# A two-layer hybrid decoder trunk: eight constants loaded after the third pair of tiles, and the first stage's small steps re-set

## The chip, the core and the metric

The kernel runs on one core of one Trainium2 chip. The metric is the device time of one execution in microseconds (us). Shown for the kernel before are three timed runs, with their median, and one further execution that was profiled.

## What is computed

```python
c_act = silu(c)
for l in range(2):                                  # DEPTH
    shift, scale, gate = split(c_act @ w_mod[l] + b_mod[l])
    h = rms_norm(x, pre_gain[l]) * (1 + scale) + shift
    proj = h @ w_in[l]          # 3088 columns: aq ak av ag | rq rk rv rg | gq gk gv gg ga
    a = window_attention(rope(aq), rope(ak), av, sinks[l]) * silu(ag)   # 8 heads, window 128
    r = rms_norm(retention(rot(rq), rot(rk), rv)) * silu(rg)           # 4 heads, chunks of 128
    g = rms_norm(gla(gq, gk, gv, log_sigmoid(ga @ gate_w + gate_b) / 16), gn) * silu(gg)
    y = concat(a, r, g) @ w_out[l]
    x = x + gate * rms_norm(y, post_gain[l])
```

x is 1 x 1024 x 1024 in fp32. All products are fp32 in accuracy.

## The kernel before, in words

The 1024 tokens are cut into eight tiles of 128 (`t` = 0 to 7), which are worked on in four pairs (`p`). An accurate fp32 product is made of three fast ones: each operand is split into a high part (rounded to fp32r) and a low part (the rest), and high x high, low x high and high x low are summed in PSUM. A projection of one tile onto one unit of weights (256 columns, or 272 for `gg`, which carries the 16 gate columns `ga`) is therefore 3 x 8 = 24 products (`accum`, L161 in the trace, since all products go through one helper).

Weights live in an arena of seven places. `load` (from L463 on) brings a unit in four chunks of 256 KB into a staging tile (`st`, five buffers), makes the high part (L145 on ScalarE or L147 on VectorE; in the first two units L484 and L488, on ScalarE) and then the low part (L491, on GpSimd or VectorE).

The first stage goes like this. The modulation of layer 0 (`mod_first`) multiplies `c_act` by two 1024 x 1024 blocks of `w_mod`, in two halves `hh` of eight steps `k`: the shift on TensorE, one row of 512 columns per step, and the scale on VectorE (L326). `finish` turns the row and the VectorE sum into columns, one small product per 128 values; for the first half that is done in the second half's step `FIN`. Meanwhile `x` tiles 0 and 1 come in over ScalarE's queue (`xk`), are squared and summed on ScalarE (L541), get their reciprocal root on GpSimd (L543 to L545, `rstd_early`), are scaled (L602), transposed on TensorE (L176), modulated (L647, L648) and split into high and low parts. The first unit `gg` is split beside this. As soon as the modulation stands, `gg` is multiplied with tiles 0 and 1 (`begin`, `complete`).

Tiles 2 and 3 come next (`pre` with `soon`): squares at L581, reciprocal root in `rstd2` (a sum at L534 and a scale at L528 on VectorE, a power at L529 on GpSimd), scaling at L600 (ScalarE) and L602 (VectorE), eight transposes a tile (L176), modulation at L622 (ScalarE) and L624 (VectorE), high part at L628 (ScalarE), low part at L629 (GpSimd for the first half of a tile, VectorE for the second). Tiles 4 to 7 follow by the same lines (`pre_first`); their `x` is loaded by the Sync queue at L686.

Then `layer(0)` runs the gates: for each pair first `gg`, then `rg` (`do_gates`). Each gate gives a SiLU (L1007 on ScalarE, L1009 on VectorE) that is written to DRAM, and `gg` also gives the gate logits (L1015, a transpose, L1024). After the gates come the decays of the gated linear attention (`gla_log`, `gla_decays`), retention, the attention projections, and the output projection; then layer 1.

Three things set the order of the work.

- On TensorE the order is the order of the program. The program is written as jobs on a planned clock: every product advances `clk`, and a job that yields `L["pf1"]` is taken up again when the clock is that many us further (`pump`, called every seven products). So the table `L` decides after how many products a transpose or a small product is put in.
- On the other engines, the Sync queue (SP) among them, a scheduler of the language picks the order: of the instructions that are ready, the one that stands first in the program. It looks over the whole program. On the chip every engine then takes its own list strictly in order.
- `tc.issue_after` pins some instructions behind another one on their engine (`XF`, `GH`).

In the kernel before, the eight constants (`causal` to `cdt`, 64 KB each for the first three, 128 KB for `rmask`, 1 to 2 KB for the others) stand in the program right behind `pump()` at L756, and the attention sinks, the gate weights `gwt` and the norm gain `gncol` stand at L795 to L808, ahead of the layers. None of them is used in the gates. The VectorE steps on them are the copies at L799 and the scaling at L808.

Of the kernel before, what the change touches and what calls it, by code (L numbers as in the profile page):

```python
# [89 lines left out]
def trunk(ctx: ExitStack, tc: tile.TileContext, ins, cst, out):  # L90
# [665 lines left out]
    pump()  # L756
    causal = cload("causal")
    mask2 = cload("mask2", I32)
    curmask = cload("curmask", I32)
    rmask = cload("rmask")  # L760
    hmask = cload("hmask")
    qdec = cload("qdec")
    kdec = cload("kdec")
    cdt = cload("cdt")
    kv = {}
# [11 lines left out]
    def gla_tiles():  # L777
# [13 lines left out]
        for b in range(2):  # L791
            gz["sc"].append([gp.tile([P, 4, 129], F32, tag="smx", name=nm("sc"), bufs=SMB)[:, :, 0:P] for _ in range(2)])
            for c in range(2):
                G.memset(gz["sc"][b][c], 0.0)
    sink8 = cp.tile([P, 2, 8], F32, name="sink8")  # L795
    sinkn = small(16)
    nc.sync.dma_start(sinkn, sinks.rearrange("(o a) b -> o (a b)", o=1).to_broadcast((P, 16)))
    for l in range(DEPTH):
        V.tensor_copy(sink8[:, l].rearrange("p (m r) -> p m r", r=2),  # L799
                      sinkn[:, 8 * l:8 * l + 8].rearrange("p (r m) -> p m r", r=2))  # L800
    gwt = cp.tile([32, 2, P], F32, name="gwt")
    V.memset(gwt, 0.0)
    for l in range(DEPTH):
        nc.sync.dma_start(gwt[0:16, l, :], gw_in[l])
        nc.sync.dma_start(gwt[16:17, l, :], gb_in[l:l + 1, :])
    for j in range(2):
        nc.sync.dma_start(gncol[64 * j:64 * j + 64, :], gn_in.rearrange("a b -> b a"))
    V.tensor_scalar(gncol, gncol, 0.5, None, ALU.mult)  # L808

# [503 lines left out]
    def layer(l):  # L1313
# [24 lines left out]
        for n in ((1, 1, 1, 1), (3, 1))[l]:  # L1338
            p0 = gates_done[l]
            for name in ("gg", "rg"):  # L1340
                for p in range(p0, p0 + n):
                    do_gates(name, p)
            if l == 0 and p0 == 0:
                load(l, "rq")
            gates_done[l] += n

        job(mod_all(l, (2,)))
# [162 lines left out]
TURN = ("AV", "AV")  # L1510
L = {"tt1": 5.71, "tt2": 6.96, "tb1": 28.02, "tb2": 0.05, "pf3": 12.62, "pf1": 6.69, "pf2": 4.0, "mod1": 4.3, "mod2": 2.4, "mod3": 17.69, "mod4": 5.8, "mod5": 0.09, "mod6": 0.05, "pre1": 7.43, "kv1": 8.84, "kv2": 2.31, "aq1": 7.17, "aq7": 7.95, "ag1": 5.62, "aq2": 2.4, "aq6": 6.2, "aq3": 11.35, "aq4": 7.54, "aq5": 4.01, "hn1": 8.14, "hn2": 3.76, "gz1": 10.47, "gz2": 13.49, "gl1": 4.43, "gd3": 16.57, "gc1": 1.21, "gc2": 1.95, "gc3": 0.65, "gc4": 3.27, "gc6": 3.2, "gc5": 4.23, "rc1": 0.73, "rc2": 2.11, "rc3": 1.31, "rc4": 2.84, "fin1": 11.68, "lay1": 0.05, "mod2@1": 2.23, "mod3@1": 16.46, "mod5@1": 3.78, "mod6@1": 3.24, "pre1@1": 10.18, "kv1@1": 3.37, "kv2@1": 0.05, "aq1@1": 5.95, "aq7@1": 6.81, "ag1@1": 8.3, "aq2@1": 2.07, "aq6@1": 9.39, "aq3@1": 11.0, "aq4@1": 6.32, "aq5@1": 1.76, "hn1@1": 10.35, "hn2@1": 3.59, "gz1@1": 3.83, "gz2@1": 12.55, "gl1@1": 17.99, "gd3@1": 15.63, "gc1@1": 1.6, "gc2@1": 1.95, "gc3@1": 0.47, "gc4@1": 1.87, "gc6@1": 0.05, "gc5@1": 1.38, "rc1@1": 0.12, "rc2@1": 3.46, "rc3@1": 2.6, "rc4@1": 5.99, "fin1@1": 9.35, "lay1@1": 1.23, "gc7": 0.81, "gc7@1": 0.33, "tb0": 0.05, "mod7": 1.0, "mod7@1": 1.0}
# [12 lines left out]
XM = (0, 3)  # L1524
LOG = (0,)
XF = 3
GH = (0,)
INP = 0
TT = 7
RG_V = ()  # L1530
FIN = 1

# [31 lines left out]
```

## Time and profile before

| | us |
|---|---|
| median of the 3 timed runs | 971.86 |
| lowest and highest of them | 971.38 and 972.01 |
| the profiled execution, its own time | 971.16 |
| its span, first to last instruction | 969.4 |

The mean granted TensorE clock of the profiled execution is 0.996. DMA moves 140.30 MB, 145 GB/s over the span.

How to read the views: a timeline row has its start and length in us, the engine, the line, the operation, the tile written and those read, the shape, how many instructions are merged into it (x), and in brackets how long the engine had been idle before it and what ended that. PE is TensorE, PEld its weight load, DVE VectorE, ACT ScalarE, POOL GpSimd; a q (SPq, ACTq) marks the engine's instruction queue, where DMAs are issued. A windows row has, for a stretch, the busy time and the number of instructions of PE, PEld, DVE, ACT and POOL, then the granted TensorE clock, the DMA share and GB/s.

### The profile page before, as it was taken

How to read it: one execution, taken by the hardware profiler on the slowest of the kernel's cores; microseconds unless marked ns; L12 is line 12 of the kernel's file. 1: busy time of each engine (PE TensorE's matmuls, PEld its weight loads, DVE VectorE, ACT ScalarE, POOL GpSimd, SP SyncE). 2: the span in 40 equal slices, each digit the busy share in tenths (PEclk: the TensorE clock that was granted, in tenths of full speed). 3: DMA queues.
4: the chain of work that ended last, by engine and by line, in shares of the span. 5: the costliest groups of instructions: out<-in, count | busy, mean ns of one | idle time of the engine just before them, and what ended most of it. 6: DMA issues, size and time to landing. Idle time of an engine off the chain costs nothing.

```text
span 969.4 us, 18061 instructions
## 1 busy us (share of the span) xinstructions
PE 951.3 (98%) x6513; PEld 829.4 (86%) x6513; DVE 640.2 (66%) x1525; ACT 410.1 (42%) x1119; POOL 272.5 (28%) x323
## 2 busy tenths in 40 slices
PE   6999999999999999999999999999999999999997
PEld 1799999989998877878889999998999887777886
DVE  6886857777777777655586485686776577763332
ACT  2777312354422666622455531134652166761111
POOL 3243011533430344511242110144423034441000
PEclk9999999999999999999999999999999999999999
DMA  9943314624335355677455160253222333555871
GB/s 313 320 146 110 111 56 129 187 77 112 115 102 150 98 168 180 218 242 237 172 166 172 50 180 22 83 155 92 80 86 77 120 88 105 158 174 174 261 238 65
DMA packets 124293, 140.30 MB, mean 145 GB/s; under 512 B 12734, under 2 KB 95528, under 8 KB 124204
## 3 DMA queue, kind: packets, MB, share of 16 engines
q1 hardware_dynamic: 116204, 127.43, 42.9%
q10 hardware_dynamic: 8000, 11.72, 3.4%
q8 instruction: 51, 0.84, 0.4%
q14 instruction: 38, 0.31, 0.1%
HBM read 102.42 MB, written 34.60 MB: 141 GB/s over the span
## 4 chain that ended last, share of the span: by engine, by line
PE 86%; DMA 7%; DVE 3%; issue 2%; POOL 1%; ACT 0%; SPq 0%; DVEq 0%; ACTq 0%; POOLq 0%
PE mm L161 67%; PE aux L161 15%; PE aux L176 4%; DMA wm<-in_w_mod_dram 2%; DMA t<-in_x_dram 1%; DMA st<-in_w_in_dram 1%; DMA xk<-in_x_dram 1%; DMA t<-aoS 1%; DMA st<-in_w_mod_dram 1%; POOL sm L529 1%; DVE acc L367 0%; DVE t L1292 0%; POOL arena L491 0%; DVE t L624 0%; DMA c_ident<-cst_ident_dram 0%
## 5 line engine op out<-in xcount | busy, mean ns | idle before, releaser
L161 PE MATMUL mm<-arena,arena 128*128 128x256 f32 (+2 forms) x1896 | 303.0, 315 | 1.4 <-ACT arena L628 0.7
L161 PE MATMUL mm<-arena 128*128 128x256 f32 (+2 forms) x1824 | 294.7, 317 | 0.0
L161 PEld LDWEIGHTS mm<-arena,arena 128*128 128x128 f32 x1896 | 261.8, 188 | 24.6 <-ACT arena L628 1.2
L161 PEld LDWEIGHTS mm<-arena 128*128 128x128 f32 x1824 | 255.4, 191 | 22.0 <-issue 1.2
L161 PE MATMUL mm<-arena,mx 128*128 128x512 f32 (+1 forms) x744 | 168.7, 386 | 0.0
L161 PEld LDWEIGHTS mm<-arena,mx 128*128 128x128 f32 x744 | 135.6, 188 | 29.1 <-issue 1.5
L529 POOL TENSOR_TENSOR sm<-sm,mhalf 128x4 f32<-128x4 f32 (+1 forms) x60 | 51.8, 863 | 294.8 <-DVE sm L528 285.3
L491 POOL TENSOR_TENSOR arena<-st,arena 128x512 fp32r<-128x512 f32 x55 | 80.3, 1467 | 91.3 <-ACT arena L145 34.7
L145 ACT ACTIVATE t<-aux 128x512 f32<-128x512 f32 (+1 forms) x96 | 48.7, 521 | 106.4 <-PE aux L176 44.9
L943 POOL TENSOR_TENSOR smx<-smx,sm 128x512 f32<-128x512 f32 x32 | 36.2, 1131 | 114.8 <-DVE sm L942 111.4
L491 DVE TENSOR_TENSOR arena<-st,arena 128x512 fp32r<-128x512 f32 x65 | 62.3, 969 | 4.7 <-PE mm L161 2.6
L145 ACT ACTIVATE arena<-st 128x512 fp32r<-128x512 f32 x82 | 48.5, 626 | 29.0 <-PE mm L161 13.0
L1247 ACT ACTIVATE t<-mm 128x512 f32<-128x512 f32 x30 | 17.9, 597 | 92.2 <-PE mm L161 40.3
L939 ACT ACTIVATE smx<-smx,sm 128x129 f32<-128x129 f32 x128 | 50.0, 393 | 14.0 <-DVE sm L936 13.9
L1248 DVE TENSOR_TENSOR t<-mm,modg 128x512 f32<-128x512 f32 x30 | 20.6, 689 | 48.6 <-ACT t L1247 48.5
L367 DVE SCALAR_TENSOR_TENSOR acc<-st,c_act,acc 128x512 f32<-128x512 f32 x60 | 47.3, 788 | 7.5 <-DMA st<-in_w_mod_dram 6.8
L1292 DVE SCALAR_TENSOR_TENSOR t<-t,sm,t 128x512 f32<-128x512 f32 x32 | 25.9, 846 | 39.7 <-DMA t<-xs 20.8
L176 PE MATMUL aux<-c_ident,t 128*128 128x128 f32 x288 | 45.5, 278 | 2.9 <-DVE t L602 2.9
L176 PEld LDWEIGHTS aux<-c_ident,t 128*128 128x128 f32 x288 | 34.9, 144 | 7.3 <-DVE t L602 4.2
L934 DVE COPY_PREDICATED smx<-c_curmask,aux 128x256 f32<-128x256 int32 x64 | 25.5, 447 | 15.0 <-ACT smx L145 10.4
L990 ACT ACTIVATE t<-aux 128x256 f32<-128x256 f32 x32 | 12.2, 382 | 54.1 <-PE aux L161 26.8
L995 DVE TENSOR_TENSOR t<-aux,sm 128x256 f32<-128x256 f32 x32 | 13.6, 425 | 30.8 <-POOL sm L529 30.8
(214 smaller groups left out, 1300.9 us busy)
## 6 DMA issues: line engine op xcount, KB each, us to landing
st<-in_w_in_dram SPq DMA_DIRECT2D x96, 256.0 KB
st<-in_w_mod_dram SPq DMA_DIRECT2D x64, 256.0 KB
mx<-mixS SPq DMA_DIRECT2D x30, 512.0 KB
mixS<-t SPq DMA_DIRECT2D x64, 128.0 KB
st<-in_w_out_dram SPq DMA_DIRECT2D x32, 256.0 KB
mixS<-t SPq DMA_DIRECT2D x32, 256.0 KB
wm<-in_w_mod_dram SPq DMA_DIRECT2D x12, 512.0 KB
t<-in_x_dram SPq DMA_DIRECT2D x24, 256.0 KB
```

What stands on the lines that cost most here:

```text
L145: A.activation(dst, src, AF.Copy)
L161: T.matmul(dst, lhsT, rhs, start=start, stop=stop)
L176: T.transpose(dst, src, idn)
L367: V.scalar_tensor_tensor(acc, wt, c_act[:, k:k + 1], acc, ALU.mult, ALU.add)
L491: i = (G if first == 0 and kc in LOG else V if first == 0 else eng(f"wlo{kc}")).tensor_tensor(wt[:, 1, 2 * kc:2 * kc + 2, 0:256], st, f(hi ...
L529: after[2] = G.tensor_tensor(r, r, mhalf[:, :w], ALU.pow)
L934: V.copy_predicated(sv, curmask.unsqueeze(1).to_broadcast((P, 2, P)), pv[:, :, n // P - 1, :])
L939: A.activation(sm[:, h, :], sm[:, h, :], AF.Exp, bias=mx[:, h:h + 1], accum_out=sums[:, h:h + 1])
L943: eng("pn").tensor_tensor(sm[:, :, 0:128], sm[:, :, 0:128], rs.unsqueeze(2).to_broadcast((P, 4, P)), ALU.mult)
L1247: A.activation(yg, pm, AF.Square, accum_out=ss[:, nh:nh + 1])
L1248: V.tensor_tensor(yg, pm, modg[l][:, 512 * nh:512 * nh + 512], ALU.mult)
L1292: V.scalar_tensor_tensor(xt[j], yg[j], r, xt[j], ALU.mult, ALU.add)
```

## The change

The constants, the sinks, `gwt` and `gncol` move into a function, `load_constants`, that is called in `layer(0)` when the gates of the third pair (`CL` = 2) have been put into the program. Inside it the sinks, `gwt` and `gncol` stand first and the eight constants after them. Beside this, single steps of the first stage change engine or place, and some planned times change.

```diff
@@ first stage @@
-    causal = cload("causal")
...
-    cdt = cload("cdt")
@@ ahead of the layers @@
-    sink8 = cp.tile([P, 2, 8], F32, name="sink8")
...
-    V.tensor_scalar(gncol, gncol, 0.5, None, ALU.mult)
+    causal = mask2 = curmask = rmask = hmask = qdec = kdec = cdt = sink8 = gwt = None
+
+    def load_constants():
+        nonlocal causal, mask2, curmask, rmask, hmask, qdec, kdec, cdt, sink8, gwt
+        sink8 = cp.tile([P, 2, 8], F32, name="sink8")
+        sinkn = small(16)
...
+        V.tensor_scalar(gncol, gncol, 0.5, None, ALU.mult)
+
+        causal = cload("causal")
...
+        cdt = cload("cdt")
@@ layer, gates @@
             gates_done[l] += n
+            if l == 0 and p0 == CL:
+                load_constants()
@@ settings @@
-L: "pf1": 6.69, "pf2": 4.0,  "mod1": 4.3,  "mod2": 2.4,  "gl1": 4.43, "gd3": 16.57, "fin1": 11.68, "fin1@1": 9.35, "lay1@1": 1.23
+L: "pf1": 7.45, "pf2": 3.96, "mod1": 6.36, "mod2": 2.46, "gl1": 4.5,  "gd3": 16.47, "fin1": 11.8,  "fin1@1": 9.47, "lay1@1": 0.46
+CL = 2
-RE = 1
+RE = 0
-RE2 = 0
+RE2 = 1
-LOG = (0,)
+LOG = (0, 1)
-GH = (0,)
+GH = ()
-RG_V = ()
+RG_V = (2, 3)
-FIN = 1
+FIN = 0
```

(The table `L` is one line in the program; only its changed entries are shown.) What the settings do:

- `RE`, `RE2`: with 1 the reciprocal root of a tile is made by three GpSimd steps (`rstd_early`), with 0 by two VectorE steps and one GpSimd step (`rstd2`); `RE` is for tiles 0 and 1, `RE2` for tiles 2 and 3.
- `LOG`: the chunks of the first unit `gg` whose low part is made on GpSimd instead of VectorE; chunk 1 joins chunk 0.
- `GH`: with tile 0 in it, the modulation of tile 2 is pinned behind the SiLU of tile 0's gate; empty, it is not.
- `RG_V`: the chunks of `rg` whose high part is made on VectorE instead of ScalarE; chunks 2 and 3 move.
- `FIN`: the step of the second half in which the first half's `finish` is done.

More of the change, by code (lines that the diff above doesn't have):

```diff
@@ L756, in trunk @@
     pump()
-    causal = cload("causal")
[L758 to L763, printed above, removed]
-    cdt = cload("cdt")
     kv = {}
@@ L794, in gla_tiles @@
                 G.memset(gz["sc"][b][c], 0.0)
-    sink8 = cp.tile([P, 2, 8], F32, name="sink8")
[L796 to L807, printed above, removed]
-    V.tensor_scalar(gncol, gncol, 0.5, None, ALU.mult)
+    causal = mask2 = curmask = rmask = hmask = qdec = kdec = cdt = sink8 = gwt = None
[3 more added lines that the diff above has]
+        sinkn = small(16)
+        nc.sync.dma_start(sinkn, sinks.rearrange("(o a) b -> o (a b)", o=1).to_broadcast((P, 16)))
+        for l in range(DEPTH):
+            V.tensor_copy(sink8[:, l].rearrange("p (m r) -> p m r", r=2),
+                          sinkn[:, 8 * l:8 * l + 8].rearrange("p (r m) -> p m r", r=2))
+        gwt = cp.tile([32, 2, P], F32, name="gwt")
+        V.memset(gwt, 0.0)
+        for l in range(DEPTH):
+            nc.sync.dma_start(gwt[0:16, l, :], gw_in[l])
+            nc.sync.dma_start(gwt[16:17, l, :], gb_in[l:l + 1, :])
+        for j in range(2):
+            nc.sync.dma_start(gncol[64 * j:64 * j + 64, :], gn_in.rearrange("a b -> b a"))
+        V.tensor_scalar(gncol, gncol, 0.5, None, ALU.mult)
+        causal = cload("causal")
+        mask2 = cload("mask2", I32)
+        curmask = cload("curmask", I32)
+        rmask = cload("rmask")
+        hmask = cload("hmask")
+        qdec = cload("qdec")
+        kdec = cload("kdec")
+        cdt = cload("cdt")
     def rotary(dst, src, nh, t, kind):
```

2 lines of the change are left out of this document (1 added, 1 removed).

## The prediction

> **What bounds the kernel now.** I read the page's span and engine rows first, then TensorE's waits, then windows, then the timeline from 32 to 80 us, engine by engine.
>
> ```profile
> span 969.4 us, 18061 instructions
> PE 951.3 (98%) x6513; PEld 829.4 (86%) x6513; DVE 640.2 (66%) x1525; ACT 410.1 (42%) x1119; POOL 272.5 (28%) x323
> ...
> PE aux L176 <- DVE smx L934: 0.5, 1, 0.5
> ...
> 35.00:40.00 5.00, 5.00 (x29) 4.99 (x29) 4.66 (x18) 4.13 (x13) 0.53 (x1) 0.66 0.98 300
> ...
> 80.00:969.00 889.00, 881.87 (x6083) 776.72 (x6082) 579.25 (x1386) 360.35 (x992) 247.64 (x285) 1.00 0.44 136
> ```
>
> TensorE is busy for 98% of the span, and from 80 us on for 881.87 of 889 us. So nothing in the first stage is worth anything unless TensorE comes through its own list sooner there, and all it wins there it keeps, if no later wait takes it back. A busy TensorE can still be a slow one: the rows of its products show that better than the share.
>
> ```profile
> 32.33 0.75 DVE L326 SCALAR_TENSOR_TENSOR t<-wm,c_act,t 128x512 f32<-128x512 f32 x1 [0.32 <-DMA wm<-in_w_mod_dram]
> ...
> 35.75 6.59 PE L161 MATMUL mm<-arena 128*128 128x272 f32 x39
> 42.17 0.63 PE L161 MATMUL mm<-arena,arena 128*128 128x256 f32 x4
> 42.95 0.91 PE L161 MATMUL mm<-arena,arena 128*128 128x256 f32 x3 [0.15 <-ACT arena L488]
> 43.69 2.07 PE L176 MATMUL aux<-c_ident,t 128*128 128x128 f32 x16
> 45.52 4.91 PE L161 MATMUL mm<-arena,arena 128*128 128x256 f32 x41
> 58.17 1.04 PE L176 MATMUL aux<-c_ident,t 128*128 128x128 f32 x8
> 58.96 3.91 PE L161 MATMUL mm<-arena,arena 128*128 128x256 f32 x31
> 64.85 2.37 PE L161 MATMUL mm<-arena,arena 128*128 128x272 f32 x17
> 67.43 0.77 PE L161 MATMUL mm<-arena,arena 128*128 128x272 f32 x4 [0.21 <-ACT arena L628]
> 68.73 0.65 PE L161 MATMUL mm<-arena,arena 128*128 128x272 f32 x3 [0.54 <-ACT arena L628]
> 69.22 1.03 PE L176 MATMUL aux<-c_ident,t 128*128 128x128 f32 x8
> ...
> 78.95 6.16 PE L161 MATMUL mm<-arena,arena 128*128 128x272 f32 x48
> ```
>
> Until 32.33 us the stage waits for the modulation weights, and the change takes none of their bytes away. Then TensorE loses time in three places. From 35.75 it runs 39 products of 272 columns in 6.59 us, where 48 of them take 6.16 us later (0.128 each, so 5.0 for 39): 1.6 us, at a granted clock of 0.66. From 42.17 to 43.69 it runs 7 products of 256 columns in 1.52 us; at 4.91/41 = 0.12 each they take 0.84: **0.68 us** lost to the high parts of `rg` chunks 2 and 3. The 16 transposes behind them take 45.52 - 43.69 = 1.83 us, where 8 take 58.96 - 58.17 = 0.79 and 69.22's group about the same: **0.2 us**. From 64.85 to 69.22 it runs 24 products of 272 columns in 4.37 us instead of 24 x 0.128 = 3.08: **1.29 us** lost to the high parts of tile 5.
>
> Now the chain behind tile 5, on the other engines.
>
> ```profile
> 35.33 0.46 SPq L232 DMA_DIRECT2D c_causal<-cst_causal_dram  x1
> ...
> 38.69 0.43 SPq L232 DMA_DIRECT2D c_qdec<-cst_qdec_dram  x1
> 39.55 5.14 SPq L686 DMA_DIRECT2D t<-in_x_dram  x8
> 44.73 0.43 SPq L232 DMA_DIRECT2D c_kdec<-cst_kdec_dram  x1
> ...
> 47.88 1.41 SPq L807 DMA_DIRECT2D gncol<-in_gla_norm_gain_dram  x2
> 48.42 0.47 DVE L799 COPY sink<-sm 128x8 f32<-128x8 f32 x2 [1.15 <-DMA sm<-in_attn_sinks_dram]
> 49.24 0.63 ACT L628 ACTIVATE arena<-t 128x512 fp32r<-128x512 f32 x1 [1.47 <-DVE t L624]
> ...
> 50.45 1.50 SPq L150 DMA_DIRECT2D st<-in_w_in_dram  x3
> ...
> 56.89 0.64 ACT L145 ACTIVATE arena<-st 128x512 fp32r<-128x512 f32 x1 [1.77 <-DMA st<-in_w_in_dram]
> 57.43 0.61 ACT L581 ACTIVATE t<-t 128x512 f32<-128x512 f32 x1
> ```
>
> VectorE stands still for 1.15 us for the sinks and then copies them for 0.47, with tile 2's last modulation behind it, so that ScalarE waits 1.47 us. ScalarE later stands still for 1.77 us for a chunk of `rq` weights, with the squares of tile 5 (57.43) behind that. Those chunks were issued from 50.45 on, behind nine small DMAs that held the Sync queue from 44.73 to 49.29.
>
> **The change part by part.** *The constants.* Six of them go ahead of the `x` loads (35.33 to 39.12), nine small DMAs behind. Moved back in the program they are last in line. What follows in the queue, the SiLU write-outs and `rq`, can start at 44.73 instead of 49.29, that is 4.6 us sooner, less what the write-outs wait for their data. The `rq` wait on ScalarE (1.77) then goes whole, and the stop on VectorE (1.15 + 0.47 = 1.62) too if the sinks land before their copies come up or the copies stand later. I take both: tile 5's chain comes up to 3.4 us sooner. It needs 1.29 to end the wait at 67.43, and 0.88 more because TensorE will itself be there sooner (next items): 2.17 in all, and is covered. If only one goes, 1.62 or 1.77 us is the whole gain.
>
> ```profile
> 39.85 0.15 DVE L528 TENSOR_SCALAR sm<-sm 128x1 f32<-128x1 f32 x1
> ...
> 40.98 1.29 POOL L491 TENSOR_TENSOR arena<-st,arena 128x512 fp32r<-128x512 f32 x1
> 41.04 1.52 DVE L602 TENSOR_SCALAR t<-mx,sm 128x512 f32<-128x512 f32 x1 [0.44 <-POOL sm L529]
> 42.28 1.14 ACT L488 ACTIVATE arena<-st 128x512 fp32r<-128x512 f32 x2
> ...
> 53.44 0.43 DVE L147 CAST arena<-st 128x512 fp32r<-128x512 f32 x1
> ...
> 65.86 0.88 DVE L602 TENSOR_SCALAR t<-t,sm 128x512 f32<-128x512 f32 x2 [0.34 <-POOL sm L529]
> ...
> 85.88 1.12 PE L161 MATMUL aux<-gaT,gwt 32*128 32x512 f32 x2
> ...
> 92.70 0.69 DVE L1064 TENSOR_TENSOR_SCAN t<-c_rmask,t 128x256 f32<-128x256 f32 x1
> ```
>
> The first uses of what is moved are the product of 85.88 (`gwt`) and the scan of 92.70 (`rmask`). Even if nothing were issued before 78.95, when the fourth pair's products start, they would have 6.9 and 13.7 us; that slack hides the later load, and where it is gone TensorE waits for `gwt`.
>
> *`RG_V`.* ScalarE makes chunks 2 and 3 of `rg` at 42.28, 1.14 us for both, behind squares of tile 3. VectorE has the same cast at 0.43 (row of 53.44), and it idles 0.44 us before 41.04. I take it that the casts are done by 42.2, when TensorE comes to them: the 0.68 goes, and ScalarE is relieved of 1.14 us, which helps the transposes' 0.2. If the casts come up behind the scaling of tile 3 instead, nothing goes: bounds 0 and 0.88.
>
> GpSimd's work lengthens VectorE's here. The scaling at 41.04 took 1.52 us with the GpSimd low part of 40.98 (1.29) running beside it, and 0.44 each (0.88 for two) at 65.86. The Trainium skill says why (SBUF — State Buffer, Who interferes with whom): VectorE's two-port operations, casts and scalings among them, share a port pair with GpSimd, and the later one is blocked for the whole of the earlier one's instruction. The trace agrees (1.52 against 0.44); the rule speaks against putting casts on VectorE while GpSimd makes `rg`'s low parts, and is a rival below.
>
> *`RE2`* takes two VectorE steps of 0.15 off a tile and puts them on GpSimd, busy for 0.53 of the 5 us to 40; *`RE`* does the reverse for tiles 0 and 1; *`LOG`* moves one low part of `gg` (1.29 us on GpSimd); *`FIN`* brings the first half's columns one product forward. The last three lie ahead of 32.33, under the weights' DMA, and the first is a few tenths off the path: I take nothing. Without that cover, `RE` costs two steps, 0.3 us. *`GH`* frees tile 2's modulation from the SiLU of tile 0: nothing on its own.
>
> *Planned times.* `pf1` puts the transposes of tiles 2 and 3 0.76 us later on the planned clock, some 6 products, where more of them are ready; tile 2's products come long behind. The others shift small products by 0.04 to 2 us of the plan at places where TensorE waits little: the largest wait it has after 80 us is 0.5 (row of L934). I take nothing, with 0.5 either way.
>
> **The sum** is 0.68 + 0.2 + 1.29 = 2.17 us. The profiled execution took 971.16 us, 1.76 outside its span, and would take 968.99. It lies 0.70 under the median of the runs, so I take the difference to the median: **969.7 us**. With 0.5 for the plan and half of the 0.88 in doubt, this case alone spans 968.9 to 970.4. A measurement of this kernel can tell about 0.2%, 1.94 us, from no change.
>
> **The rivals.**
>
> *The chain does not come sooner.* The program's order is only a rank: a step with nothing to wait for is pulled forward whatever its place. For it speaks that the memset below, from the attention of hundreds of us later, ran at 3.13.
>
> ```profile
> 3.13 0.53 POOL L909 MEMSET smx<- 128x512 f32 x1
> ...
> 34.91 5.33 DMA st<-in_w_in_dram
> ...
> 37.62 0.75 DVE L681 TENSOR_TENSOR arena<-t,arena 128x256 fp32r<-128x256 f32 x2
> ```
>
> So the constants may fill the same holes in the Sync queue, and the change then does not do what it says, or one of the two stops stays. TensorE then wins 0.88 at 42 us and loses it again at 67: 971.9 with neither stop gone, 970.2 with one. Against it: `rq` outranks them now. Chance 0.24.
>
> *Casts blocked by GpSimd* (the port rule above). Each cast could wait a whole low part, 1.29 us: the 0.88 stays lost and only the 1.29 is won, 970.6. Chance 0.07.
>
> *Slower: VectorE meets the sinks too early.* The sinks now stand first in `load_constants`. If they take `causal`'s place at 35.33, they land behind the last `rg` chunk (34.91 + 5.33 = 40.24). If their copies stand in VectorE's list ahead of the low parts of tiles 0 and 1 (37.62), VectorE stops for up to 40.24 - 37.62 = 2.6 us, TensorE misses those low parts at once, and nothing at 67 comes back: 974.5. It decides if the copies' place lies before about 39 us. Chance 0.11.
>
> *The half-rate stretch moves.* At 35.75 TensorE loses 1.6 us to the granted clock. If it ran at full rate there, 969.7 - 1.6 = 968.1. Against it: the work ahead of it, which sets the clock, hardly changes. Chance 0.05. The Trainium skill (TensorE: Matmul & The Clock Gate, Part 1) says that the clock follows the activity in windows of 3.4 us that do not start with the kernel; the 0.66 over 5 us agrees with one such window at half rate (1 - 0.5 x 3.4 / 5 = 0.66).
>
> **How the numbers follow.** The forecast has 0.53, and 0.40 of it lies under 969.92, the bound of 0.2%; with the clock's 0.05 that gives 0.45 for faster. The other 0.13 of it, the chain (0.24), the casts (0.07) and 0.01 of the sinks' case, where the stop is short, give 0.45 for no change. The rest of the sinks' case gives 0.10 for slower. The range reaches from about the clock's case, 968.2, to 972.3, which is no gain at all and 0.4 for the plan; it leaves out the slower rival and a little below. Most of the cases of any weight lie on one side of no change, so no second range stands beside it.
>
> **What would show it.** Right: no wait of TensorE on L488 or L628 before 80 us; `rq` chunks issued before 50 us; no idle VectorE ahead of L799 before 70 us; the product of 85.88 at about 83.7. Wrong: constants still issued between 35 and 39 us; a VectorE stop on the sinks or `gncol` before 45 us (then slower); the casts of `rg` taking over 1 us; or a start of the gates' last pair that is 2 us sooner with an end that is not, which would put a new wait behind 85.88 us.

## The result, and the profile after

| | us |
|---|---|
| changed kernel, median of 22 runs (lowest and highest) | 973.88 (972.25 to 977.48) |
| kernel before, 22 runs beside them | 971.89 (969.77 to 974.18) |
| ratio, with its 95% interval | 1.0022 (1.0014 to 1.0030) |
| the profiled execution of the changed kernel, its own time and span | 972.25 and 970.5 |

The change makes the kernel slower by 0.22%, about 2 us, where 969.7 us was forecast, and the time lies above the range. A difference of two ratios below carries the intervals of both, about 1.2 us and up to 2; a step smaller than that is not settled by the times alone. In the changed kernel the lines behind the first stage have moved by a few numbers: L1007 is L1012, L1009 is L1014, L1015 is L1020, L1024 is L1029, L799 is L795, and L486 is the new cast of `rg` on VectorE.

First the timeline of TensorE in the changed kernel: start, length, engine, line, operation, and in brackets the idle time before and what ended it.

```profile
18.60 1.75 PE L176 MATMUL aux<-c_ident,t 128*128 128x128 f32 x8 [3.44 <-DVE t L602]
22.05 1.97 PE L176 MATMUL aux<-c_ident,t 128*128 128x128 f32 x8 [1.71 <-DVE t L602]
...
35.53 1.27 PE L161 MATMUL mm<-arena 128*128 128x272 f32 x8
...
38.50 5.45 PE L161 MATMUL mm<-arena 128*128 128x272 f32 x40
45.26 2.17 PE L161 MATMUL mm<-arena,arena 128*128 128x256 f32 x14 [1.31 <-ACT arena L488]
...
53.45 2.80 PE L161 MATMUL mm<-arena 128*128 128x272 f32 x21
...
68.03 3.28 PE L161 MATMUL mm<-arena,arena 128*128 128x272 f32 x24
...
80.89 6.16 PE L161 MATMUL mm<-arena,arena 128*128 128x272 f32 x48
...
87.81 1.12 PE L161 MATMUL aux<-gaT,gwt 32*128 32x512 f32 x2
```

And the rows of the kernel before that answer to the first ones, which the prediction did not look at:

```profile
17.67 1.09 PE L176 MATMUL aux<-c_ident,t 128*128 128x128 f32 x8 [2.52 <-DVE t L602]
19.13 1.97 PE L176 MATMUL aux<-c_ident,t 128*128 128x128 f32 x8 [0.36 <-DVE t L602]
...
32.55 1.27 PE L161 MATMUL mm<-arena 128*128 128x272 f32 x8
...
35.51 6.82 PE L161 MATMUL mm<-arena 128*128 128x272 f32 x40
```

The loss comes early and is partly given back. Tile 0's transposes start 0.9 us later (18.60 against 17.67), tile 1's 2.9 us later (22.05 against 19.13), and the first products with `gg` 3.0 us later (35.53 against 32.55). The 40 products behind them run in 5.45 us instead of 6.82, because this execution has no half-rate stretch there, but TensorE then waits 1.31 us for the high part of an `rg` chunk, and the two cancel. The second pair starts 3.2 us late (53.45 against 50.26). From there the change wins: the 24 products of tile 5 take 3.28 us without a wait, and the last pair starts 1.94 us late (80.89 against 78.95), as does the product with `gwt` (87.81 against 85.88). That agrees with the 2 us of the medians; the two profiled executions themselves end 1.1 us apart, since 0.8 us is caught up between 165 and 950 us.

### The profile page after: what moved, and what is told of

Same layout as the page of the kernel before. It is cut to its first block, busy times and chain, and to the rows that moved or that the text cites. A ratio compares the mean times of both kernels' runs of the same rounds, so it can differ in the third digit from the quotient of the medians.

```text
span 970.5 us, 18053 instructions
## 1 busy us (share of the span) xinstructions
PE 950.3 (98%) x6513; PEld 828.7 (85%) x6513; DVE 641.7 (66%) x1526; ACT 408.2 (42%) x1117; POOL 272.5 (28%) x324
## 4 chain that ended last, share of the span: by engine, by line
PE 93%; DMA 2%; DVE 2%; issue 1%; POOL 1%; ACT 0%; SPq 0%; DVEq 0%; ACTq 0%; POOLq 0%
PE mm L161 73%; PE aux L161 15%; PE aux L176 5%; DMA t<-in_x_dram 1%; DMA wm<-in_w_mod_dram 1%; DMA posi<-in_positions_dram 0%; POOL sm L529 0%; DVE t L602 0%; DMA rows<-in_b_mod_dram 0%; DVE t L1297 0%; POOL arena L491 0%; DVE arena L491 0%; DVEq L1567 0%; ACT t L145 0%; ACTq L232 0%
## 5 line engine op out<-in xcount | busy, mean ns | idle before, releaser
L529 POOL TENSOR_TENSOR sm<-sm,mhalf 128x4 f32<-128x4 f32 (+1 forms) x60 | 51.9, 866 | 306.3 <-DVE sm L528 299.6
```

The costliest lines, as they stand in the source:

```text
L529: after[2] = G.tensor_tensor(r, r, mhalf[:, :w], ALU.pow)
```

## The experiments

Two names in what follows: the kernel before with one thing changed, and the changed kernel with one thing put back. Each was run beside the kernel before on the same chip, and the ratio is to that; it differs a little from the quotient of the two medians shown.

| run | median us | before beside it | ratio (95%) |
|---|---|---|---|
| changed, `RE = 1` | 970.34 | 971.43 | 0.9987 (0.9979 to 0.9995) |
| before, `RE = 0` | 974.94 | 971.43 | 1.0030 (1.0016 to 1.0043) |
| changed, root on GpSimd for tile 1 only | 971.59 | 971.74 | 0.9997 (0.9989 to 1.0006) |
| changed, root steps ahead in VectorE's list | 971.71 | 972.11 | 0.9997 (0.9984 to 1.0010) |
| the same, `FIN = 1` | 970.90 | 972.11 | 0.9989 (0.9978 to 0.9999) |
| changed, `RE = 1`, `FIN = 1` | 970.12 | 971.74 | 0.9981 (0.9972 to 0.9989) |
| before, constants moved | 973.20 | 971.43 | 1.0018 (1.0008 to 1.0029) |
| the same, one SiLU held | 972.51 | 971.74 | 1.0007 (0.9996 to 1.0018) |
| the same, `rq` held too | 971.68 | 972.16 | 0.9991 (0.9980 to 1.0002) |
| changed, constants in their old place | 978.39 | 971.43 | 1.0069 (1.0053 to 1.0084) |
| the same, `GH = (0,)` | 975.78 | 972.16 | 1.0042 (1.0026 to 1.0058) |
| before, `RG_V = (2, 3)` | 973.64 | 972.16 | 1.0014 (1.0004 to 1.0024) |
| changed, `RE = 1`, `FIN = 1`, `RG_V = ()` | 974.30 | 972.11 | 1.0016 (1.0006 to 1.0025) |
| changed, `RE = 1`, `RE2 = 0`, both holds | 971.43 | 972.16 | 0.9992 (0.9981 to 1.0002) |
| before, 18 unused products | 972.15 | 971.74 | 1.0007 (0.9995 to 1.0020) |

### Is it `RE`?

The theory from the two traces is that `RE = 0` costs the 3 us: the root of tiles 0 and 1 goes through VectorE, whose list is busy with the weight sums of the modulation. Rivals are `FIN` (the weight sums of a whole half stand behind `finish`) and the constants. First `RE` by itself, once put back in the changed kernel and once put into the kernel before.

```diff
 # the changed kernel
-RE = 0
+RE = 1
```

> The changed kernel with one setting put back: RE = 1, so the reciprocal roots of tiles 0 and 1 are made by three GpSimd steps again. Theory (VectorE's queue): in the changed kernel the two VectorE steps of a root stand behind weight steps that wait for DMA, so tile 1's transposes start at 22.05 instead of 19.13 us and the modulation ends 3 us later; put back, they start before 20 us and the kernel is 1.5 to 3 us faster than the changed one, at or under the kernel before (969.5 to 972). Rival (FIN): the first half's columns, done one step earlier, stop VectorE and TensorE; then this kernel stays within 0.7 us of the changed one. Rival (constants): the moved DMAs cost the time; then it also stays there.

```diff
 # the kernel before
-RE = 1
+RE = 0
```

> The kernel before with one setting of the change: RE = 0. Theory (VectorE's queue): tile 1's transposes start about 2 to 3 us later, the gates start 1 to 3 us later, and the kernel is 1 to 3 us slower than the kernel before. Rival (FIN) and rival (constants): within 0.7 us of the kernel before, since neither is touched.

Measured: 970.34 us (ratio 0.9987) and 974.94 us (ratio 1.0030). `RE = 0` costs 0.35% in the new settings (1.0022 against 0.9987, 3.4 us) and 0.30% in the old ones (2.9 us). All the rest of the change together is worth a gain of 0.13%.

Then by tile, with the root of tile 1 alone on GpSimd:

```diff
-        r = rstd_early(xt, to) if early and RE or soon and RE2 else rstd2(squares(xt, to))
+        r = rstd_early(xt, to) if early and t in RE or soon and RE2 else rstd2(squares(xt, to))
...
-RE = 0
+RE = (1,)
```

> The changed kernel with the early reciprocal root on GpSimd for tile 1 alone; tile 0 keeps its two steps on VectorE. Theory 'VectorE's queue': tile 0's transposes come 0.9 us later than in the kernel before, tile 1's 2.9, and the weight row waits for the later of the two; so tile 1 sets the time, and nearly all of the 3.5 us comes back: 970.3 to 971.3. If both tiles' steps cost alike, each about half: about 972.1. If tile 0's wait just moves on to tile 1, nothing comes back: 973.9.

Measured: 971.59 us, ratio 0.9997. Of the 0.35%, 0.25% is tile 1's (2.4 us) and 0.10% tile 0's (1.0 us, which is within the interval of a difference). The traces agree: the first products with `gg` start at 35.53 us in the changed kernel, at 32.92 here and at 32.10 with `RE = 1` for both tiles. Tile 1 has most of it, but less than nearly all, which was expected.

What takes the time? VectorE and GpSimd in the changed kernel, from the root of tile 0 to the scaling of tile 1:

```profile
16.08 0.75 DVE L326 SCALAR_TENSOR_TENSOR t<-wm,c_act,t 128x512 f32<-128x512 f32 x1 [1.10 <-DMA wm<-in_w_mod_dram]
16.75 0.15 DVE L528 TENSOR_SCALAR sm<-sm 128x1 f32<-128x1 f32 x1
...
18.06 0.88 DVE L602 TENSOR_SCALAR t<-xk,sm 128x512 f32<-128x512 f32 x2 [0.44 <-POOL sm L529]
18.86 0.15 DVE L534 TENSOR_TENSOR sm<-sm 128x1 f32<-128x1 f32 x1
...
19.26 0.14 DVE L528 TENSOR_SCALAR sm<-sm 128x1 f32<-128x1 f32 x1
...
20.51 1.88 DVE L602 TENSOR_SCALAR t<-xk,sm 128x512 f32<-128x512 f32 x2 [0.45 <-POOL sm L529]
```

```profile
16.97 1.05 POOL L529 TENSOR_TENSOR sm<-sm,mhalf 128x1 f32<-128x1 f32 x1 [13.33 <-DVE sm L528]
19.48 0.99 POOL L529 TENSOR_TENSOR sm<-sm,mhalf 128x1 f32<-128x1 f32 x1 [1.46 <-DVE sm L528]
20.45 1.26 POOL L491 TENSOR_TENSOR arena<-st,arena 128x512 fp32r<-128x512 f32 x1
```

The first rows are tile 0's, the later ones tile 1's. The second step of tile 0's root (L528, 0.15 us) stands behind a weight sum that stands still 1.10 us for its transfer. The first step of tile 1's (L534 at 18.86) stands behind tile 0's scaling, though ScalarE had tile 1's squares done by 15.43. In the kernel before the roots were done by 15.86 and 18.43, by these GpSimd rows:

```profile
15.31 0.55 POOL L545 TENSOR_TENSOR sm<-sm,mhalf 128x1 f32<-128x1 f32 x1
...
17.75 0.68 POOL L545 TENSOR_TENSOR sm<-sm,mhalf 128x1 f32<-128x1 f32 x1
```

In the changed kernel L529 is also longer than L545 was, there is one more hop between engines, and tile 1's scaling, now beside the GpSimd low part at 20.45, takes 1.88 us for two where tile 0's takes 0.88. To tell the place in the list from the hop, the steps were left on VectorE and only put ahead of the weight sums; `issue_after` sets the place and adds no wait of its own:

```diff
-        V.tensor_scalar(r, ss, scale, eps, ALU.mult, ALU.add)
+        roots.append(V.tensor_scalar(r, ss, scale, eps, ALU.mult, ALU.add))
...
-                    mark[2] = V.scalar_tensor_tensor(acc, wm[1][:, k], c_act[:, k:k + 1], acc, ALU.mult, ALU.add)
+                    with ExitStack() as es:
+                        for m in roots[:2] if hh == 0 and k > 3 else ():
+                            es.enter_context(tc.issue_after(m.ins))
+                        mark[2] = V.scalar_tensor_tensor(acc, wm[1][:, k], c_act[:, k:k + 1], acc, ALU.mult, ALU.add)
...
+    roots = []
```

> The changed kernel as it is, RE = 0 with the root's two steps on VectorE, but with the weight sums of half 0 from k = 4 on held behind the root steps of tiles 0 and 1 in VectorE's list. Theory 'VectorE's queue': what RE costs is the place of the two steps behind a weight sum that waits for its DMA; with the steps ahead of it tile 1's transposes come at about 19.5 us instead of 22.05 and nearly all of the 3.4 us between 973.88 and 970.34 comes back: 970.3 to 971.3. Rival 'the hop': the cost is the way from VectorE to GpSimd and back and the root itself (1.05 and 0.99 us instead of 0.55 and 0.68); then tile 1 comes at about 21 us and half stays: 972 to 973. If the held weight sums come late themselves and the weight row with them: 974 or more.

> The same with FIN = 1. Theory 'VectorE's queue': as without it, within 0.5 us, since FIN alone moved the time by 0.06% at most: 970 to 971.3. If FIN = 0 hides the held weight sums, this one is over 1 us slower than the other.

Measured: 971.71 us (0.9997), and with `FIN = 1` 970.90 us (0.9989). VectorE in the first of the two (its lines are shifted: L531 is L528, L606 is L602):

```profile
17.38 0.15 DVE L531 TENSOR_SCALAR sm<-sm 128x1 f32<-128x1 f32 x1
...
18.63 0.88 DVE L606 TENSOR_SCALAR t<-xk,sm 128x512 f32<-128x512 f32 x2 [0.45 <-POOL sm L532]
```

```profile
19.17 1.97 PE L176 MATMUL aux<-c_ident,t 128*128 128x128 f32 x8 [1.82 <-DVE t L606]
...
33.87 1.27 PE L161 MATMUL mm<-arena 128*128 128x272 f32 x8
```

With the same steps on the same engines tile 1's transposes are back at 19.17 us, where the kernel before has them, and 0.25% of the 0.35% is back (with `FIN = 1`, 0.33% of the 0.41% that `RE` and `FIN` together give back below). So most of what `RE` costs comes from the place in VectorE's list. What is left is within the interval of a difference; it can be the hop, or the clock: in this execution `gg` starts at 33.87, 1.3 us later than in the kernel before although tile 1 is as early, and the granted clock from 20 to 25 us is 0.50. The first value lies 0.4 us above what was expected.

`FIN` was also put back beside `RE`:

```diff
 # the changed kernel
-RE = 0
+RE = 1
...
-FIN = 0
+FIN = 1
```

> The changed kernel with RE and FIN as before (1 and 1), all else new. With RE alone it took 970.34 us. Rival 'FIN': the seven weight sums of half 0 stand behind the last finishing step in VectorE's list and cost TensorE 0.5 us or more before 32 us; then 969.8 or less. Theory 'VectorE's queue' gives FIN nothing: 970.3, within 0.5. A time over 971 would say that FIN = 0 helps.

Measured: 970.12 us, 0.9981 against 0.9987 without it: not told apart, and it rules `FIN` out as the cause of the loss. This version has the lowest time of all that were run, not told apart from `RE = 1` alone, and is faster than both kernels.

### What are the constants worth?

The kernel before with only the constants moved:

```diff
 # the kernel before; all settings as they were
-    causal = cload("causal")
...
+            if l == 0 and p0 == CL:
+                load_constants()
```

> The kernel before with the constants, sinks, gwt and gncol moved as in the change, and nothing else: all settings and planned times are the old ones. Theory (VectorE's queue), with the prediction's chain: the stops on the sinks and on the rq weights go, the 1.29 us wait at tile 5 goes, and the kernel is 0.5 to 2 us faster than before. Rival (constants): 1 us or more slower than before. Rival (FIN): says nothing of it, faster by the same 0.5 to 2.

Measured: 973.20 us, ratio 1.0018. The expected gain is not there; alone the move costs 1.75 us. ScalarE and then VectorE show why. ScalarE in this kernel:

```profile
51.59 0.38 ACT L1012 ACTIVATE t<-mm 128x256 f32<-128x256 f32 x1 [4.45 <-PE mm L161]
51.87 1.85 ACT L622 ACTIVATE t<-aux,mod,mod 128x128 f32<-128x128 f32 x5
```

The SiLU of the first `rg` tile (51.59) now stands ahead of tile 2's modulation (51.87). It waits 4.45 us for its product while the modulation, ready long before, stands behind it. In the kernel before the modulation comes first (44.77). The length of this wait is not the usual one: the execution took 976.09 us, 2.9 over the median of its kind, and from 45 to 50 us, under the products that the SiLU waits for, the granted clock is 0.50. The next run holds that SiLU in its old place:

```diff
-                    dma("ssr", srS[t], silu2(pg[:, 0:256]))
+                    with ExitStack() as es:
+                        if l == 0 and t == 0:
+                            es.enter_context(tc.issue_after(turned[2].ins))
+                        sg = silu2(pg[:, 0:256])
+                    dma("ssr", srS[t], sg)
```

> The kernel before with the constants moved, and the SiLU of rg tile 0 held back behind tile 2's last high part, the order that ScalarE's list had before the move. The move alone took 973.2 us against 971.43. Theory 'list order': the move's loss is that SiLU, which waits 4.45 us for its product while tile 2's modulation stands behind it on ScalarE; held back, gg of the second pair ends about 50 us instead of 54.3 and the loss goes, to 971.5 or less; with the predicted gain of the SP chain (1.3 us at tile 5) 970.1. If the loss is the waits on the rg high parts (1.51 and 0.66), it stays: about 973.

Measured: 972.51 us, 1.0007: of the loss of 0.18%, 0.11% is gone, not all of it, and that step alone is within the interval of a difference. VectorE in this run shows what else is out of order:

```profile
43.48 0.41 DVE L147 CAST arena<-st 128x512 fp32r<-128x512 f32 x1
43.93 0.69 DVE L491 TENSOR_TENSOR arena<-st,arena 128x512 fp32r<-128x512 f32 x1
44.54 0.15 DVE L534 TENSOR_TENSOR sm<-sm 128x1 f32<-128x1 f32 x1
...
45.95 1.49 DVE L602 TENSOR_SCALAR t<-mx,sm 128x512 f32<-128x512 f32 x1 [0.45 <-POOL sm L529]
```

L147 at 43.48 is a cast of `rq`, weights that are used after all gates. With the constants out of the Sync queue its transfer came in early, and the scheduler put the cast and its low part, 1.1 us, ahead of tile 3's root (L534, L528). Tile 3's scaling comes at 45.95 where the kernel before has it at 43.49. So the next run holds `rq` too:

```diff
             if l == 0 and p0 == 0:
-                load(l, "rq")
+                with tc.issue_after(scaled[3].ins): load(l, "rq")
```

> The kernel before with the constants moved, the SiLU of rg tile 0 held as in the run with that hold alone (972.51 against 971.74 of before), and the loads and casts of rq held behind the scaling of tile 3. In that run a cast of rq and its low part stood ahead of tile 3's root in VectorE's list, so that TensorE waited 1.67 and 0.66 us around 44 us. Theory 'list order': with both steps back in their old places, the move shows only the gain that was predicted of it, the 1.29 us wait on tile 5's high parts: 970.0 to 971.2. Rival 'the early loads themselves cost' (rq's transfers ahead of the x loads, whatever the lists): still 972 to 973.

Measured: 971.68 us, 0.9991; the time is 0.5 us above what was expected, the kernel before beside it 0.7 us slower than beside the first runs. Up to 68 us only VectorE's list differs from that of the run above. TensorE's waits at this place are now 0.15 and 0.49 us, and tile 5 has none:

```profile
43.72 0.91 PE L161 MATMUL mm<-arena,arena 128*128 128x256 f32 x3 [0.15 <-ACT arena L488]
...
48.97 3.00 PE L161 MATMUL mm<-arena,arena 128*128 128x256 f32 x24 [0.49 <-DVE t L1014]
...
66.39 3.26 PE L161 MATMUL mm<-arena,arena 128*128 128x272 f32 x24
```

From 1.0018 to 0.9991 in two steps that only reorder lists: that the move's loss is in the orders is shown, for the two steps together. What remains is a gain of 0.09%, whose interval reaches no change. That does not contradict the 1.29 us that the prediction took for tile 5, but neither does it show them: TensorE comes to tile 5 1.5 us later here than in the kernel before, and a later TensorE finds no wait there with the constants in their old place either (see the constants in the part on the prediction).

In the new settings the same move has another worth. The changed kernel with the constants in their old place:

```diff
 # the changed kernel; the calls back at their place ahead of the layers
+    causal = cload("causal")
...
-            if l == 0 and p0 == CL:
-                load_constants()
```

> The kernel before with all settings and planned times of the change, but the constants at their old place. Theory (VectorE's queue): the loss stays and the gain of the chain goes, so it is slower than the kernel before by 2 to 4 us and not faster than the changed kernel. Rival (constants): the loss goes, within 0.7 us of the kernel before. Rival (FIN): as the theory.

Measured: 978.39 us, 1.0069. It is 0.47% (4.5 us) slower than the changed kernel, much more than was expected. TensorE waits longest here:

```profile
54.74 4.48 PE L161 MATMUL mm<-arena,arena 128*128 128x256 f32 x24 [2.56 <-DVE t L1009]
```

With `GH = ()` the SiLU of the first two `gg` tiles stands behind tile 2's modulation, and this is late itself. Put back:

```diff
-GH = ()
+GH = (0,)
```

> The changed kernel with the constants where they were before (978.39 us, 6.7 over before), and GH = (0,), which holds tile 2's modulation behind gla logits of tile 0. Theory 'list order': with GH = () and the constants early, the SiLU steps of gg tiles 0 and 1 stand behind tile 2's modulation, which stands behind the sinks, and TensorE waits 2.56 us for a free PSUM bank; with GH = (0,) this wait goes and the time is 975.0 to 976.5. If that wait is only the visible end of the stop on the sinks and on rq, another takes its place: 978.

Measured: 975.78 us, 1.0042. The wait of 2.56 us is gone and the time with it, 0.27%, as expected. The remaining 0.42% over the kernel before is near the 0.35% of `RE`; it was not taken apart further.

### `RG_V` and `RE2`

The prediction's largest term of the sum at 42 us was `RG_V`, 0.88 us. By itself in the kernel before:

```diff
 # the kernel before
-RG_V = ()
+RG_V = (2, 3)
```

> The kernel before with RG_V = (2, 3) alone; the lists differ from before by the two casts that go from ScalarE to VectorE, with the low part of chunk 2 behind them ahead of tile 3's root. By the prediction the waits on rg chunks 2 and 3 (0.68) and at the transposes (0.2) go: 970.9. Theory 'list order': the casts end the wait on the chunks, but tile 3's root and scaling come about 1.4 us later in VectorE's list, so the wait moves to tile 3's transposes and nothing is won: 971.7 to 972.5.

Measured: 973.64 us, 1.0014: slower by 1.4 us. TensorE, VectorE and GpSimd of this run:

```profile
43.78 0.72 PE L161 MATMUL mm<-arena,arena 128*128 128x256 f32 x3 [1.49 <-DVE arena L486]
...
47.44 1.09 PE L176 MATMUL aux<-c_ident,t 128*128 128x128 f32 x8 [2.06 <-ACT t L600]
48.29 6.52 PE L161 MATMUL mm<-arena,arena 128*128 128x256 f32 x41
```

```profile
41.90 1.49 DVE L602 TENSOR_SCALAR t<-mx,sm 128x512 f32<-128x512 f32 x1 [0.44 <-POOL sm L529]
43.31 0.75 DVE L486 CAST arena<-st 128x512 fp32r<-128x512 f32 x2
...
44.58 1.22 DVE L534 TENSOR_TENSOR sm<-sm 128x1 f32<-128x1 f32 x1
```

```profile
44.14 1.64 POOL L491 TENSOR_TENSOR arena<-st,arena 128x512 fp32r<-128x512 f32 x1 [1.03 <-DVE arena L486]
```

The casts are as short as was said (0.75 for two), but they stand behind the scaling of tile 2, so TensorE waits 1.49 us for them where it lost 0.68 us to ScalarE; and tile 3's root stands behind them, so that it waits 2.06 us more at tile 3's transposes. The theory of the expectation said that the first wait would end; it did not, and both are there.

In the new settings it is the other way round:

```diff
 # the changed kernel with RE = 1, FIN = 1
-RG_V = (2, 3)
+RG_V = ()
```

> The changed kernel with RE, FIN and RG_V as before (1, 1, no casts on VectorE). With RE and FIN alone it took 970.12 us (ratio 0.9981). RG_V alone made the kernel before 1.4 us slower, because tile 3's root came behind the casts in VectorE's list. Theory 'list order': with RE2 = 1, tile 3's root is on GpSimd and not behind the casts, so RG_V costs less here than there, and without it ScalarE has 1.14 us more ahead of the transposes: 970 to 971. If RG_V costs the same here, this version is the best of all: 968.7.

Measured: 974.30 us, 1.0016, where 970 to 971 was expected, or 968.7. Without `RG_V` the version with `RE` and `FIN` put back loses 0.35%. ScalarE and TensorE:

```profile
44.28 1.65 ACT L488 ACTIVATE arena<-st 128x512 fp32r<-128x512 f32 x3
```

```profile
44.94 2.25 PE L161 MATMUL mm<-arena,arena 128*128 128x256 f32 x12 [1.45 <-ACT arena L488]
47.00 3.57 PE L176 MATMUL aux<-c_ident,t 128*128 128x128 f32 x16
```

With `RE2 = 1` the squares of tiles 2 and 3 stand ahead of all four chunks on ScalarE. If ScalarE has all four casts then, three of them run from 44.28, and TensorE waits 1.45 us for them; `RG_V` takes two of them off it. But the wait is hardly longer than the 1.31 us of the changed kernel, and the 16 transposes take 3.57 us because the granted clock is 0.50 from 47 to 50 us. This execution, at 975.18 us, was the slowest of its kind. So the 3.4 us are measured, and this trace does not show how they come about. As measured the two settings belong together: `RG_V` without `RE2` is a loss, and `RE2` without `RG_V` is one too.

The last of this group takes `RE2` back and holds both list places of the section above:

```diff
 # the changed kernel
-RE = 0
+RE = 1
...
-RE2 = 1
+RE2 = 0
 # and the two holds of the runs above
```

> The changed kernel with RE = 1 and RE2 = 0 as before, and the SiLU of rg tile 0 and the casts of rq held as in the other run of this call. With RE = 1 alone it took 970.34 us and TensorE waited 1.33 us at 42 us for the high part of an rg chunk that stands on ScalarE behind the squares of tile 3. With RE2 = 0 ScalarE makes chunks 0 and 1 before them. Theory 'list order': most of that wait goes, 968.8 to 969.8. If VectorE, which gets two root steps back per tile, is late in its place: 970.3 to 971.5.

Measured: 971.43 us, 0.9992. The expected gain is not there. VectorE, with the two steps per tile back and the two casts as well, is late here, as the rival of the expectation said; TensorE waits for it twice:

```profile
42.90 1.55 PE L161 MATMUL mm<-arena,arena 128*128 128x256 f32 x10 [1.49 <-DVE arena L486]
...
46.58 1.09 PE L176 MATMUL aux<-c_ident,t 128*128 128x128 f32 x8 [1.26 <-ACT t L600]
```

The second wait names L600 on ScalarE, but both it and VectorE's scaling wait for the root, whose first steps stand behind the casts.

### The clock

Between the profiles lies one more difference: the stretches in which TensorE is granted half of its clock. In the kernel before one such stretch lay at 36 to 39 us; in the changed kernel there was none there, and it ran the 40 products of 38.50 in 5.45 us. But both have an earlier one, on the transposes and the products of the modulation, and in the changed kernel it is longer. The kernel before and then the changed one (busy time and number of instructions of PE, PEld, DVE, ACT and POOL, then the granted clock):

```profile
20.00:25.00 5.00, 5.00 (x14) 1.33 (x12) 4.96 (x8) 1.96 (x4) 1.58 (x2) 0.77 1.05 361
```

```profile
20.00:25.00 5.00, 3.29 (x12) 1.78 (x11) 4.55 (x6) 1.01 (x3) 3.69 (x4) 0.50 1.05 366
```

Over all windows from 17 to 45 us the two profiles lose nearly the same to it, by estimate 3.4 and 3.5 us of full rate, so it is not what sets these two executions apart. To see whether the median hangs on such stretches, unused products were put in TensorE's idle time ahead of tile 0's transposes (they are added to the computation and nothing reads them):

```diff
 # the kernel before
+            idle = mm()
+            for i in range(18):
+                T.matmul(idle[:, 0:128], ones, ones, start=i == 0, stop=i == 17)
```

> The kernel before with 18 unused fp32 products 128x128x128 of constants in TensorE's idle time ahead of tile 0's transposes. They add work that the reference does not have, and nothing reads them. Theory 'clock': half-rate stretches in the first stage (two of 3.4 us in the profiled run, about 1.6 us each where TensorE has work) come from TensorE standing still before 17 us, and differ from execution to execution; kept busy there, the median falls by 0.5 to 1.5 us and the spread of 4 us gets narrower. If the stretches come whatever stood before, or if they cost nothing on the path, the time stays at 971.4 and the spread at about 4 us. If the dummies push the transposes out, it gets slower by as much as they last, 1 to 3 us.

Measured: 972.15 us (970.61 to 978.37), 1.0007: no gain, and no narrower spread. The windows of this run:

```profile
17.00:20.00 3.00, 3.00 (x30) 3.00 (x29) 2.45 (x5) 0.72 (x2) 1.18 (x3) 1.00 1.14 337
20.00:25.00 5.00, 5.00 (x30) 2.76 (x29) 5.00 (x10) 2.05 (x4) 2.04 (x2) 1.00 1.05 361
25.00:35.00 10.00, 9.34 (x38) 3.64 (x37) 8.45 (x15) 4.87 (x12) 0.00 (x0) 1.00 1.06 381
35.00:40.00 5.00, 5.00 (x32) 4.97 (x31) 4.83 (x15) 4.09 (x11) 0.53 (x1) 0.71 0.93 293
```

The clock is full up to 35 us here, and the stretch behind it (0.71 from 35 to 40) comes all the same. The products also push tile 0's transposes to 20.53 us, 2.9 us later than before, so that a gain and a loss can both be in the 972.15: what the early clock alone is worth stays open.

A rival inside the cost of `RE` stays open with it. The granted clock of every timed execution is on record, and its mean goes with `RE`: 0.994 in the changed kernel and 0.998 with `RE = 1`, 0.992 in the kernel before with `RE = 0` and 0.997 without. An estimate from these: 0.004 of 970 us is 3.9 us of full rate, as much as `RE` costs. A late root may therefore cost twice: TensorE starts later, and more of what it then runs is at half rate. The trace of the kernel before with `RE = 0` has both: tile 1's transposes start 4.0 us later (23.14 against 19.13) and `gg` 5.3 us later (37.82 against 32.55), with a granted clock of 0.50 from 20 to 25 us and 0.79 from 25 to 35. How the loss divides between the two is not shown; no run kept TensorE busy ahead of these transposes in the changed kernel.

## Why the prediction was wrong

**The step that failed** is the one on `RE`: "The last three lie ahead of 32.33, under the weights' DMA [...] I take nothing. Without that cover, `RE` costs two steps, 0.3 us." It costs 2.9 to 3.4 us. It went wrong in two places.

First, the cover was read from the wrong engine. "Until 32.33 us the stage waits for the modulation weights" rested on a VectorE row with 0.32 us of idle time. Grouped by line, the products of the modulation on TensorE from tile 1's transposes on (the window 19 to 33 us of the kernel before: count, busy us, mean ns, idle us before them) say something else:

```profile
L161 PE MATMUL mm<-wm,c_act 128*1 128x512 f32 x20 | 9.7, 625 | 0.0
```

No idle time shows ahead of the products. Some of their weight loads do name the transfer as what they waited for. The longest is the last:

```profile
31.60 0.09 PEld L161 LDWEIGHTS mm<-wm,c_act 128*1 128x1 f32 x2 [0.95 <-DMA wm<-in_w_mod_dram]
```

It costs about 0.2 us, by estimate: the 12 products from 27.13 to 32.55 take 5.4 us, where the 14 of the changed kernel take 6.1. Behind tile 1's transposes TensorE has 13.4 us of work in its own order (32.55 - 19.13), and the same 13.5 us in the changed kernel (35.53 - 22.05); both hold half-rate time. So what delays tile 1 delays `begin` by as much, and the cover is thin. With `RE = 1` in the changed kernel, which ran at full rate there, tile 1 comes at 18.66, and there TensorE itself waits for the weights, 0.79 and later 0.34 us; `gg` starts at 32.10, only 0.45 us sooner than in the kernel before.

```profile
18.66 1.09 PE L176 MATMUL aux<-c_ident,t 128*128 128x128 f32 x8 [0.36 <-DVE t L602]
...
22.34 1.02 PE L161 MATMUL mm<-wm,c_act 128*1 128x512 f32 x2 [0.79 <-DMA wm<-in_w_mod_dram]
```

Second, the price without the cover was the length of the two steps, 0.15 us each. What they cost is the work ahead of them in VectorE's list: a weight sum that stands 1.10 us for its transfer, tile 0's scaling, and behind them a scaling that then falls together with a GpSimd low part. Time at half clock may be in it too, as said above.

**`RG_V`**: its 0.88 us did not come. The prediction's other bound ("if the casts come up behind the scaling of tile 3 instead, nothing goes") was nearer, but its floor was zero: alone, it cost 1.4 us. In the changed kernel TensorE waits 1.31 us at 45.26 for another chunk, since `RE2` puts the squares ahead of chunks 0 and 1 on ScalarE. That coupling was not in the text, which took `RE2` for "a few tenths off the path".

**The constants**: the term for tile 5 came out in size, in part by luck. ScalarE no longer stands still for `rq`, VectorE no longer for the sinks, and the 24 products take 3.28 us; between the second and the last pair's start the changed kernel wins 1.25 us (80.89 - 53.45 = 27.44 against 78.95 - 50.26 = 28.69), where 1.29 was said. But a TensorE that comes 3 us later can win that anyhow: in the kernel before with `RE = 0` alone, and with `RG_V` alone, the constants are in their old place, and the 24 products take 3.26 us without a wait too (at 71.88 and 69.18). What speaks for the chain is the changed kernel with `RE = 1`: there they start at 64.61, no later than the 64.85 of the kernel before, and take 3.26 us. How much of that is the constants alone is not shown. What was missed is that the freed queue would not only be empty: `rq` moved up into it, and its cast and the SiLU of a gate went ahead of steps that were due. In the old settings that turns the gain into a loss of 1.75 us.

**The sign to watch**: no wait on L628 and no idle time ahead of the sinks' copies came true; no wait on L488 did not, with `RE = 1` either (1.33 us there). Of `rq` only the first chunk was issued before 50 us (38.10), the other three from 51.49 on, and the product with `gwt` came at 87.81 instead of 83.7, both behind the 3 us of `RE`.

**The rivals**: the eight constants did move (to 56.51 and later; only two small pieces of `gwt` still went at 39.23 and 39.74), the casts were not blocked by whole low parts, and VectorE met the sinks at 78.08 without a stop, so the loss was not the one named for the slower side. The half-rate stretch did go away from 36 us, but its 1.6 us were not won: TensorE, 1.37 us sooner, waited 1.31 us on ScalarE. So it had been hidden.

**`LOG`, `GH` and the planned times** were not tested one by one in the settings they had; with the constants, `RE2`, `RG_V` and `FIN` they make up the gain of 0.13%. How it divides among them is open.

## What to carry to other kernels

Before an edit is costed at nothing "under the DMA", look at the engine that comes through last in that stretch, here TensorE: if none of its own rows waits, nothing is covered there. The price of a small step moved to another engine is what stands ahead of it in that engine's list, and of a step that is taken away, what the scheduler pulls into the gap; so compare the lists of all engines, not the durations. A wait in an execution that ran well over its median, or at half clock in that place, is not the usual wait. Settings that share one engine's list are tried together: `RG_V` was worth -1.4 us in one setting and +3.4 us in another, and the constants' move -1.75 and +4.5.

## What the runs showed of the hardware

- A VectorE step on one column, L534, took 1.22 us instead of 0.15 beside a GpSimd low part. It began at 44.58 and ended at 45.80; the low part of 44.14 ended at 45.78. The Trainium skill (SBUF — State Buffer, Who interferes with whom) says that a VectorE instruction with two inputs in SBUF contends with a GpSimd instruction that reads SBUF, and that the one that comes second is fully blocked; these rows agree to 0.02 us. So the length of a small step says little about what it takes beside a long one.
- Half-rate stretches of TensorE's clock also come behind work that is dense by the page: with 18 unused products the clock is 1.00 from 17 to 35 us with TensorE busy for 17.34 of 18 us, and then 0.71 from 35 to 40. And they come behind waits: after the 2.06 us in the `RG_V` run 41 products took 6.52 us, 0.159 each, where 0.12 is full speed. The Trainium skill (TensorE: Matmul & The Clock Gate, Part 1) lets the clock fall after an idle window of about 3.4 us; neither of these two has so long an idle time by the profile, so here the measurement does not fit, and what counts as idle stays open.
